# SSD steps hung beside the products of U, and y_a, s_out and w_o as a dense stage of their own

## The chip, the cores and the metric

The kernel runs on one core of one Trainium2 chip. The metric is the device time of one execution in microseconds. Before the change three runs took 2009.54, 2010.28 and 2015.11 us, a median of 2010.28 us.

TensorE is called PE below, VectorE DVE, ScalarE ACT and GpSimd POOL. SP is the engine whose queue issues all DMAs of this kernel, one after the other, in program order.

## The reference

One layer of a hybrid decoder block on 1024 tokens with 1024 channels, all in float32:

```python
u  = rmsnorm(h)
gate_a, gate_s, b_a, c_a, v_a, z, xbc, dt_raw = split(u @ w_in)
y_a = (b_a * causal_dwconv(c_a * v_a, conv_a_w)) @ w_a_out
xbc = silu(causal_dwconv(xbc, ssd_conv_w) + ssd_conv_b)
xs, bs, cs = split(xbc)
y   = ssd_chunked_scan(xs, dt, a, bs, cs) + d_skip * xs
y_s = group_rmsnorm(y * silu(z), ssd_norm_w) @ w_s_out
h   = h + (sigmoid(gate_a) * y_a + sigmoid(gate_s) * y_s) @ w_o
v   = rmsnorm(h)
h1, h3 = split(v @ w_up)
h   = h + (silu(causal_dwconv(h1) + b) * h3) @ w_down
out = rmsnorm(h)
```

The scan works in chunks of 128 tokens: within a chunk it multiplies the products of b and c by a lower triangular decay matrix exp(a_cum[l] - a_cum[s]) for each head; between chunks it carries a state of 64 x 128 per head. There are 32 heads of 64 channels in 4 groups, so 8 heads share a group's b and c. The group norm divides by the root mean square over the 512 channels of a group.

## The kernel before

**Products.** Each large product is made of float32 values that are split in a high part and a rest (`split` L136, `wsplit` L141: ACT casts the high part, POOL or DVE subtracts it for the low part). `product` (L240) accumulates hi x hi, hi x lo and lo x hi in one PSUM bank: twelve matmuls of 128x512. `Pair` (L252) multiplies two 128-column blocks of a weight with the operand U (later V) by a seven-product scheme: b11, b21, t1, t2, t3, t4, b22, so a pair is 84 matmuls. Raw weights come through four buffers (`load` L146, tag raw); split weights through 14 buffers of the tag w and four of wx.

**PSUM.** Eight banks: four have the name "mm" (`mm_tile`), four "sd" (`sd_tile`). Of a pair's products t1, t4 and b22 use sd, and so does every small product of the scan. A bank is free again when DVE or ACT has read it. The additions of a pair into its two results (L274 to L304) are on DVE.

**Order.** A tile scheduler takes program order as priority and places instructions on each engine's queue; an engine then executes its queue in order.

**Stages.** The row norms of x and the filling of U come first (`u_norm`, `fill_first`). Then come the pairs of U: xbc with its four-tap convolution on DVE (L508) and z, both stored to DRAM (`ssd_in`); then `ca_pairs` and the gates. Between those, `m_preps` calls `m_prep` 32 times, once for each group and chunk: it loads b and c (bc), forms their product pb (L585, in an sd bank), masks it on DVE (L587), forms the decays on ACT (Relu with a bias for each of 8 heads L591, Exp L592), multiplies both on DVE (L593) and stores the 128x1024 matrix to DRAM (md).

Then `steps` and `fill` weave 32 calls of `ssd_chunk`, each a generator of four pieces, with y_a and s_out. A chunk loads x, b, c, z (in) and the decay matrix (m), transposes x and b on PE (px L658, pb L660), scales them (xd L662 on DVE, xe L669 on ACT), and multiplies: pd = m x xd (L686), po = state x c (L696), pst = b x xe (L705). DVE and POOL sum y (L700 to L702) and the new state (L710, L714), DVE multiplies by z (L717), ACT squares (L718), and a product with a matrix of ones sums the squares (pn L723). Then a square root (L725), a reciprocal (L726), four scalings (L729) and the split into yh and yl follow, which s_out reads. `s_out` adds each group's product to sacc on DVE (L783).

`merge` joins both branches by the gates, `out_proj` (L853) multiplies by w_o and adds into h (L879). `v_norm` stores h to DRAM (hd), norms it, and `fill_first` and `fill_second` transpose it into V (pt_v, L176). The FFN's pairs then run; beside the first eleven, `w_sums` forms sums of w_down (tiles wd, L932) and stores them (td).

## Time and profile before

| | before |
|---|---|
| median of three runs | 2010.28 us |
| profiled execution | 2007.71 us |
| its span | 2006.0 us |
| mean granted TensorE clock | 0.986 of full |
| PE busy | 1923.7 us, 96% |
| DVE busy | 1395.0 us, 70% |
| POOL busy | 1215.7 us, 61% |
| ACT busy | 880.7 us, 44% |
| DMA | 346.84 MB, mean 173 GB/s |

The profiled execution lasts 1.71 us longer than its span, which runs from the first to the last instruction. Busy times are sums of an engine's instructions; a busy PE need not be at its peak, since matmuls overlap and their ends are modelled. A view by stretches shows for a piece of the span how long each engine was busy and with how many instructions. A row of waits names the engine that idled, the tile and line that it was about to work on, and the instruction that it waited for. Most tables and rows are quoted where the prediction uses them.

### The profile page before, as it was taken

What the parts mean: (1) busy time and instruction counts of PE and PEld (TensorE: products, weight loads), DVE (VectorE), ACT (ScalarE), POOL (GpSimd) and SP (SyncE); (2) the same over time, 40 slices, a digit from 0 to 9 for tenths busy, and PEclk for the clock granted to TensorE, in tenths of its full rate; (3) what the DMA queues carried; (4) which work ended last, traced back from release to release, by engine and by line L of the source; (5) the groups of instructions that cost most, each with busy time, mean ns of one, the idle gap of its engine ahead of it and who ended that gap; (6) DMA issues with size and microseconds to landing.
All of it is one profiled execution on the core that took longest, in us unless ns stands there. A gap on an engine that the chain in (4) does not pass through costs nothing. (4 is left out here: it accounts for less than half of the span.)

```text
span 2006.0 us, 26149 instructions
## 1 busy us (share of the span) xinstructions
PE 1923.7 (96%) x8978; PEld 1574.4 (78%) x8978; DVE 1395.0 (70%) x1732; ACT 880.7 (44%) x1676; POOL 1215.7 (61%) x895
## 2 busy tenths in 40 slices
...
GB/s 142 79 152 103 131 97 124 103 107 119 188 209 204 229 187 183 227 219 204 209 184 169 190 146 194 234 142 164 195 245 208 113 163 148 149 242 276 215 181 145
DMA packets 203573, 346.84 MB, mean 173 GB/s; under 512 B 14896, under 2 KB 111664, under 8 KB 203440
## 3 DMA queue, kind: packets, MB, share of 16 engines
...
## 5 line engine op out<-in xcount | busy, mean ns | idle before, releaser
L674 POOL TENSOR_TENSOR xs<-in,dsk 128x512 f32<-128x512 f32 x32 | 34.9, 1091 | 177.9 <-DMA in<-ssd_in 117.3
L508 DVE SCALAR_TENSOR_TENSOR cv<-xbc,scw,cv 128x1024 f32<-128x1024 f32 x72 | 109.8, 1551 | 15.8 <-ACT cv L504 15.8
L591 ACT ACTIVATE mp<-mp,tk 128x128 f32<-128x128 f32 x256 | 78.5, 389 | 93.4 <-DMA mp<-acd 79.5
L508 DVE SCALAR_TENSOR_TENSOR fcv<-fci,fcw,fcv 128x1024 f32<-128x1024 f32 x44 | 74.5, 1693 | 23.8 <-ACT fcv L504 23.6
L669 ACT ACTIVATE xe<-px,tk 128x64 f32<-128x64 f32 x256 | 56.1, 331 | 57.4 <-DVE xd L662 57.4
L246 PE MATMUL so<-yh,h_ws 128*128 128x512 f32 x256 | 77.0, 413 | 0.0
L246 PE MATMUL so<-yh,l_ws 128*128 128x512 f32 x256 | 73.2, 402 | 0.0
L246 PE MATMUL so<-yl,h_ws 128*128 128x512 f32 x256 | 73.2, 401 | 0.0
L593 DVE TENSOR_TENSOR mp<-mp,bc 128x1024 f32<-128x1024 f32 x32 | 51.8, 1620 | 27.7 <-ACT mp L592 27.6
L139 POOL TENSOR_TENSOR l_wo<-raw_wo,h_wo 128x512 fp32r<-128x512 f32 x24 | 37.4, 1566 | 39.0 <-PE so L246 25.5
L702 POOL TENSOR_TENSOR eb<-eb,xs 128x512 f32<-128x512 f32 x28 | 38.3, 1369 | 34.8 <-DVE eb L700 24.4
L246 PEld LDWEIGHTS so<-yl,h_ws 128*128 128x128 f32 x256 | 47.7, 188 | 12.6 <-issue 3.3
L246 PEld LDWEIGHTS so<-yh,l_ws 128*128 128x128 f32 x256 | 47.4, 188 | 11.9 <-issue 2.6
L246 PEld LDWEIGHTS so<-yh,h_ws 128*128 128x128 f32 x256 | 46.7, 188 | 12.6 <-issue 4.6
L718 ACT ACTIVATE xs<-eb 128x512 f32<-128x512 f32 x32 | 20.4, 639 | 74.3 <-DVE eb L717 74.3
L874 PE MATMUL wo<-h_wo,mh 128*128 128x512 f32 x128 | 50.3, 395 | 2.1 <-DVE sacc L783 0.8
L876 PE MATMUL wo<-h_wo,ml 128*128 128x512 f32 x128 | 50.1, 396 | 0.0
L875 PE MATMUL wo<-l_wo,mh 128*128 128x512 f32 x128 | 50.0, 392 | 0.0
L282 POOL TENSOR_TENSOR t1up<-raw_2up,raw_1up 128x512 f32<-128x512 f32 x22 | 36.7, 1666 | 17.3 <-DMA raw_2up<-in_w_up 10.9
L138 ACT CAST h_t4up<-t2up 128x512 fp32r<-128x512 f32 x22 | 13.7, 621 | 73.2 <-POOL t2up L300 46.6
L729 DVE SCALAR_TENSOR_TENSOR eb<-eb,wns,yr 128x128 f32<-128x128 f32 x128 | 44.8, 411 | 0.3
L981 ACT ACTIVATE fcv<-fcv 128x1024 f32<-128x1024 f32 x22 | 23.4, 1062 | 49.3 <-DVE fcv L508 49.3
...
## 6 DMA issues: line engine op xcount, KB each, us to landing
...
mp<-acd SPq DMA_DIRECT2D x32, 512.0 KB, 4.8
md<-mp SPq DMA_DIRECT2D x32, 512.0 KB, 3.0
m<-md SPq DMA_DIRECT2D x32, 512.0 KB, 5.0
ssd_in<-cv SPq DMA_DIRECT2D x24, 512.0 KB, 4.4
raw_wo<-in_w_o SPq DMA_DIRECT2D x24, 512.0 KB, 4.4
raw_1up<-in_w_up SPq DMA_DIRECT2D x22, 512.0 KB, 3.9
raw_2up<-in_w_up SPq DMA_DIRECT2D x22, 512.0 KB, 3.4
```

The lines of the kernel that those rows point to most:

```text
L139: (eng or pool).tensor_tensor(lo, v, f32(hi), op=ALU.subtract)
L246: pe.matmul(ps, wt[:, k, :], ct[:, k, :], start=(start and n == 0), stop=(stop and n == 11),)
L282: pool.tensor_tensor(self.t1, self.r2[:, :HALF], b11, op=ALU.subtract)
L508: dve.scalar_tensor_tensor(cv, ci[:, j : j + SEQ], w[:, j : j + 1], cv, op0=ALU.mult, op1=ALU.add)
L591: act.activation(m[:, h, :], m[:, h, :], AF.Relu, bias=a)
L593: dve.tensor_tensor(m, m, cb.unsqueeze(1).to_broadcast([P, HG, P]), op=ALU.mult)
L669: act.activation(xe[:, hc], px[:, hc], AF.Copy, scale=tk[:, 2, cc, q, g * HG + h : g * HG + h + 1],)
L702: pool.tensor_tensor(y, y, xs, op=ALU.add)
L729: dve.scalar_tensor_tensor(o, o, wns[:, 4 * g + j : 4 * g + j + 1], r, op0=ALU.mult, op1=ALU.mult)
L874: pe.matmul(pss[t], mh, wh, start=k == 0, stop=False)
L875: pe.matmul(pss[t], mh, wl, start=False, stop=False)
L876: pe.matmul(pss[t], ml, wh, start=False, stop=k == NK - 1)
```

## The change

**Steps beside the pairs.** `tick()` counts the products of pairs; `ssd_chunk` is cut into five pieces (loads, decay, transposes, the products, the norm's sum), and each piece of step s hangs at the product 11 + 6 s - 8, - 6, - 4, 0 or + 3, counted from the ninth pair. 29 of the pairs (BESIDE) run so, eight (BEFORE) ahead of them. **Decays in place.** The decay matrix is formed in a step, in the tile that the step reads; `m_prep` and md go. pc is the product of b and c that was pb in `m_prep`. **Rows in DRAM.** y goes to DRAM (yd) before the norm, and the norm's factor, one number a token and group, to rd. `y_half` loads both and scales while it fills s_out's operand. **Dense stage.** y_a, s_out and w_o run for each half of the tokens; s_out sums the four groups in one PSUM bank, and w_a_out and w_s_out (in another layout) are loaded once for each half. **w_sums** no longer lies in the FFN; in program order it stands beside s_out(0) and y_a(1). v takes a raw buffer, and the tag w has 11 buffers.

```diff
-NRAW, NW, NWX, NBIG, NB4, NC2, NT2, NROW = 4, 14, 4, 14, 3, 6, 3, 6
+NRAW, NW, NWX, NBIG, NB4, NC2, NT2, NROW = 4, 11, 4, 14, 3, 6, 3, 6
...
-XBC = (16, 18, 20, 22, 0, 2, 4, 6, 8, 10, 12, 14)
-Z_AFTER = (16, 18, 22, 0, 4, 6, 10, 12)
-PREP_CV, PREP_G = 3, 2
-YA = (0, 1, 2, 3, 4, 6, 8, 9)
-SLAG, LAST = 10, 31
+BEFORE = (
+    ("xb", 16), ("z", 0), ("xb", 18), ("z", 2), ("xb", 20), ("xb", 22), ("xb", 0), ("xb", 2),
+)
+BESIDE = (
+    ("xb", 4), ("z", 4), ("xb", 6), ("z", 6), ("ca", 0), ("ca", 1), ("ba", 0),
+    ("xb", 8), ("z", 8), ("xb", 10), ("z", 10), ("ca", 2), ("ca", 3), ("ba", 2),
+    ("xb", 12), ("z", 12), ("xb", 14), ("z", 14), ("ca", 4), ("ca", 5), ("ba", 4),
+    ("ca", 6), ("ca", 7), ("ba", 6), ("gs", 0), ("gs", 2), ("gs", 4), ("gs", 6), ("ga", 6),
+)
+D0, DSTEP = 11, 6
+LOADS, DECAY, TRANS, NORM = -8, -6, -4, 3
...
             product(ps, self.A[c], wsplit(v, f"{nm}{name}", eng, tag))
+            tick()
             return ps
...
+    slots, clock = {}, [None]
+    def tick():
+        if clock[0] is not None:
+            clock[0] += 1
+            for f in slots.pop(clock[0], ()):
+                f()
...
-    md = dram.tile([NG * NCH, P, SEQ], F32, name="md")
+    yd = [dram.tile([P, 4, SEQ], F32, name=f"yd{g}") for g in range(NG)]
+    rd = dram.tile([NG, NCH, P], F32, name="rd")
...
-            m_preps(PREP_CV)
...
-    def ssd_chunk(g, c, yh, yl):
+    states, stats = {}, {}
+    def ssd_chunk(s):
...
-        m = s4(f"m{nm}")[:, :SEQ]
-        sp.dma_start(m, md[g * NCH + c])
...
+        inp = ssp.tile([P, 6, P], F32, tag="in", name=f"in{nm}", bufs=2)
+        sp.dma_start(inp, xd_[g][:, 0:6, ts])
+        xt, bt, ct = inp[:, 0:4, :], inp[:, 4, :], inp[:, 5, :]
+        yield
+        m = ssp.tile([P, HG, P], F32, tag="m", name=f"m{nm}", bufs=1)
+        sp.dma_start(m, acd[hq, lq].unsqueeze(0).to_broadcast([P, HG, P]))
+        eb = c2(f"eb{nm}")
...
+        zt = ssp.tile([P, 4, P], F32, tag="z", name=f"zt{nm}", bufs=1)
+        sp.dma_start(zt, xd_[g][:, 6:10, ts])
+        for h in range(HG):
+            a = tk[:, 0, cc, q, g * HG + h : g * HG + h + 1]
+            act.activation(m[:, h, :], m[:, h, :], AF.Relu, bias=a)
+        act.activation(m, m, AF.Exp, scale=-1.0)
+        yield
 
...
+        pc = sd_tile(f"pc{nm}")[:, :P]
+        pe.matmul(pc, bt, ct, start=True, stop=True)
...
-        bk = row(f"bk{nm}", P)
+        bk = ssp.tile([P, P], F32, tag="bk", name=f"bk{nm}", bufs=1)
         act.copy(bk, pb)
+        cb = ssp.tile([P, P], F32, tag="cb", name=f"cb{nm}", bufs=1)
+        dve.tensor_tensor(cb, pc, tri, op=ALU.mult)
+        dve.tensor_tensor(m, m, cb.unsqueeze(1).to_broadcast([P, HG, P]), op=ALU.mult)
         yield
...
+        dve.tensor_tensor(xt, xt, tiles(pd), op=ALU.add)
+        if st is not None:
+            dve.tensor_tensor(eb, po, eb, op=ALU.mult)
+            pool.tensor_tensor(xt, xt, tiles(eb), op=ALU.add)
...
+        dve.tensor_tensor(xt, xt, zt, op=ALU.mult)
+        sp.dma_start(yd[g][:, :, ts], xt)
+        sq = eb
+        act.activation(sq, xt.rearrange("p j l -> p (j l)"), AF.Square)
+        dve.tensor_tensor(sq[:, : 2 * P], sq[:, : 2 * P], sq[:, 2 * P :], op=ALU.add)
+        dve.tensor_tensor(sq[:, :P], sq[:, :P], sq[:, P : 2 * P], op=ALU.add)
         yield
-        pn = sd_tile(f"pn{nm}")[:, :P]
-        pe.matmul(pn, ones, xs[:, :P], start=True, stop=True)
-        r = row(f"yr{nm}", P)
-        act.activation(r, pn, AF.Sqrt, scale=1.0 / HALF, bias=epsc)
-        dve.reciprocal(r, r)
-        for j in range(4):
-            o = tiles(y)[:, j, :]
-            dve.scalar_tensor_tensor(
-                o, o, wns[:, 4 * g + j : 4 * g + j + 1], r, op0=ALU.mult, op1=ALU.mult
-            )
-        split(tiles(y), yh[:, :, cs], yl[:, :, cs], dve)
+        pn = sd_tile(f"pn{nm}")[:, :1]
+        pe.matmul(pn, sq[:, :P], ones[:, :1], start=True, stop=True)
+        rs = tiny(f"yss{nm}")
+        dve.tensor_scalar(rs, pn, 1.0 / HALF, EPS, op0=ALU.mult, op1=ALU.add)
+        r = tiny(f"yr{nm}")
+        pool.tensor_tensor(r, rs, nhalf, op=ALU.pow)
+        sp.dma_start(rd[g, c].unsqueeze(1), r)
         yield
...
+    def at(n, f):
+        slots.setdefault(n, []).append(f)
+    NS = NG * NCH
+    for s in range(NS):
+        d = D0 + DSTEP * s
+        ch = ssd_chunk(s)
+        for o in (LOADS, DECAY, TRANS, 0, NORM):
+            at(d + o, lambda ch=ch: next(ch))
...
+    for item in BEFORE:
+        run(*item)
+    clock[0] = 0
+    for item in BESIDE:
+        run(*item)
+    while slots:
+        tick()
+    clock[0] = None
+    mixer.close()
...
+    def w_sums(k):
+        r, r2 = (s4(f"wd{f}{k}")[:, :SEQ] for f in range(2))
+        for f, t in enumerate((r, r2)):
+            sp.dma_start(t, w_down[f * KF + k])
+        b11, b12 = (r[:, h] for h in halves)
+        b21, b22 = (r2[:, h] for h in halves)
+        sub(b11, b12, b11)
...
+    def y_a(hf, ta, beside):
+        sl = halves[hf]
+        for j in range(NK):
+            raw = load(w_a_out[j], f"wa{hf}{j}")
+            ps = mm_tile(f"ya{hf}{j}")
             for q in range(2):
-                product(ps, ta[hf, q], ws[q], start=q == 0, stop=q == 1)
-            gh = t2(f"ga{j}{hf}")
+                w = wsplit(raw[:, halves[q]], f"wa{hf}{j}{q}", pool if q else dve)
+                product(ps, ta[q], w, start=q == 0, stop=q == 1)
...
+            beside(j)
+    def y_half(hf, res):
+        for g in range(NG):
+            rb = c2(f"rb{hf}{g}")
+            sp.dma_start(
+                rb,
+                rd[g].rearrange("c p -> (c p)")[halves[hf]].unsqueeze(0).to_broadcast([P, HALF]),
+            )
+            hi, lo = big_tile(f"yh{hf}{g}", F32R), big_tile(f"yl{hf}{g}", F32R)
+            res.append((hi, lo))
+            for j in range(0, 4, 2):
+                raw = load(yd[g][:, j : j + 2, halves[hf]], f"y{hf}{g}{j}").rearrange(
+                    "p (k t) -> p k t", k=2
+                )
+                for i in range(2):
+                    w = wns[:, 4 * g + j + i : 4 * g + j + i + 1]
+                    dve.scalar_tensor_tensor(
+                        raw[:, i, :], raw[:, i, :], w, rb, op0=ALU.mult, op1=ALU.mult
+                    )
+                split(raw, hi[:, j : j + 2, :], lo[:, j : j + 2, :], dve)
+                yield
+    def s_out(hf, ys, beside):
...
+            ps = mm_tile(f"so{hf}{j}")
+            for kk in range(2):
+                raw = load(w_s_out[kk * NK + j], f"ws{hf}{j}{kk}")
+                for i in range(2):
+                    g = 2 * kk + i
+                    w = wsplit(raw[:, halves[i]], f"ws{hf}{j}{g}", pool if i else dve)
+                    product(ps, ys[g], w, start=g == 0, stop=g == NG - 1)
+            gs, ma = c2(f"gs{hf}{j}"), c2(f"ma{hf}{j}")
+            sp.dma_start(gs, gsd[:, j, sl])
+            sp.dma_start(ma, mad[:, j, sl])
+            dve.scalar_tensor_tensor(gs, gs, 1.0, ps, op0=ALU.add, op1=ALU.mult)
+            dve.tensor_tensor(gs, gs, ma, op=ALU.add)
+            hi, lo = mg[j // 4]
+            split(gs, hi[:, j % 4, :], lo[:, j % 4, :])
+            beside(j)
+        return mg
...
     def v_norm(t):
         sp.dma_start(hd[t], hs[t])
-        v = b4(f"v{t}")
+        v = wp.tile([P, DM], F32, tag="raw", name=f"v{t}", bufs=NRAW)
...
+    def all_sums():
+        for k in range(KF):
+            w_sums(k)
+            yield
+    def beside(*gens):
+        return lambda j: [next(g, None) for g in gens]
+    sums = all_sums()
+    ta0, ta1, ys0, ys1 = [], [], [], []
+    for _ in ta_half(0, ta0):
+        pass
+    y_a(0, ta0, beside(y_half(0, ys0)))
+    mg0 = s_out(0, ys0, beside(ta_half(1, ta1), sums))
+    y_a(1, ta1, beside(y_half(1, ys1), sums))
     load_x(0)
-    out_proj(mg, 0, 4)
-    for n in range(LAST + 4, LAST + 8):
-        steps(n)
-        fill(n)
-    mg = merge(1)
+    out_proj(mg0, 0, 4)
+    def fill_beside(j):
+        if j % 2 == 0:
+            fill_first(V, v_norm(j // 2), j // 2, f"v{j // 2}")
+    V = operand("v")
+    mg = s_out(1, ys1, fill_beside)
...
-            w_sums(i)
```

Three places show how the rows moved on the engines. The first is PE around one SSD step. Before, in the scan of group 2, where so is a product of s_out:

```order
L246 MATMUL so100_9228<-yl10_8117,h_ws100_9224 128x512 x4
L705 MATMUL pst2_1_9202<-xe2_1_9082,bk2_1_9093 128x512
L246 MATMUL so100_9228<-yh10_8116,l_ws100_9225 128x512 x4
L246 MATMUL so101_9242<-yh14_8571,h_ws100_9224 128x512 x4
L246 MATMUL so101_9242<-yl14_8572,h_ws100_9224 128x512
L723 MATMUL pn2_0_9211<-xs2_0_8996,ones_662 128x128
L246 MATMUL so101_9242<-yl14_8572,h_ws100_9224 128x512 x3
```

After, group 0's second step among the products of an xbc pair of U:

```order
L256 MATMUL pt1xb6_2755<-us1h_301,l_t1xb6_2757 128x512 x4
L682 MATMUL pd0_1_2772<-m0_1_2589,xd0_1_2657 64x128 x8
L689 MATMUL po0_1_2781<-in0_1_2527,st0_2582 128x128 x4
L695 MATMUL pst0_1_2786<-xe0_1_2659,bk0_1_2669 128x512
L256 MATMUL pt2xb6_2814<-us2h_303,h_t2xb6_2815 128x512 x4
L256 MATMUL pt2xb6_2814<-us2l_304,h_t2xb6_2815 128x512 x4
L256 MATMUL pt2xb6_2814<-us2h_303,l_t2xb6_2816 128x512 x4
L256 MATMUL pt3xb6_2835<-us3h_305,h_t3xb6_2836 128x512 x4
L256 MATMUL pt3xb6_2835<-us3l_306,h_t3xb6_2836 128x512 x4
L256 MATMUL pt3xb6_2835<-us3h_305,l_t3xb6_2837 128x512 x4
L651 MATMUL px0_2_2852<-ident_75,in0_2_2727 128x128 x4
L653 MATMUL pb0_2_2857<-ident_75,in0_2_2727 128x128
```

The step's products pd, po and pst now stand in one piece between two products of a pair, and the next step's transposes follow two products later.

The second place is SP's queue where the last rows of h are stored (hd from h4 and h6) and weights of w_o (raw_wo) and of the FFN (raw_1up, raw_2up) are loaded. Before:

```order
L148 DMA raw_wo161_11834<-in_w_o 128x1024
L889 DMA hd_96<-h4_11348 128x1024
L148 DMA raw_wo162_11856<-in_w_o 128x1024
L889 DMA hd_96<-h4_11348 128x1024
L148 DMA raw_wo163_11878<-in_w_o 128x1024
L148 DMA raw_1up0_11922<-in_w_up 128x1024
L148 DMA raw_2up0_11961<-in_w_up 128x1024
L148 DMA raw_1up1_12031<-in_w_up 128x1024
L148 DMA raw_2up1_12070<-in_w_up 128x1024
L889 DMA hd_96<-h6_11350 128x1024 x2
```

After:

```order
L158 DMA raw_wo143_11774<-in_w_o 128x1024
L898 DMA hd_100<-h4_11600 128x1024 x2
L158 DMA raw_wo060_11818<-in_w_o 128x1024
L158 DMA raw_wo061_11840<-in_w_o 128x1024
L158 DMA raw_wo062_11862<-in_w_o 128x1024
L158 DMA raw_wo063_11884<-in_w_o 128x1024
L158 DMA raw_wo160_11972<-in_w_o 128x1024
L158 DMA raw_wo161_11994<-in_w_o 128x1024
L158 DMA raw_wo162_12016<-in_w_o 128x1024
L158 DMA raw_wo163_12038<-in_w_o 128x1024
L898 DMA hd_100<-h6_11602 128x1024 x2
L158 DMA raw_1up0_12082<-in_w_up 128x1024
```

Both stores of h4 now stand ahead of the weights wo06 and wo16, and both stores of h6 ahead of the FFN's first weight.

The third place is POOL in the last gate pairs (names with g) after the change:

```order
L149 TENSOR_TENSOR l_t2g10_8261<-t2g10_8239,h_t2g10_8260 128x512
L763 TENSOR_TENSOR wd00_9531<-wd10_9532,wd00_9531 128x512
L311 TENSOR_TENSOR t2g10_8239<-t2g10_8239,raw_1g10_8188 128x512
L724 TENSOR_TENSOR yr3_2_8006<-yss3_2_8004,nhalf_80 128x1
L763 TENSOR_TENSOR wd10_9532<-wd10_9532 128x512
L149 TENSOR_TENSOR l_t3g10_8324<-t3g10_8320,h_t3g10_8323 128x512
```

The sums of w_down (wd, L763) stand there among the splits of a gate pair and the scan's rows; before, all of them stood beside the FFN.

More of the change, by code (lines that the diff above doesn't have):

```diff
@@ L349, in tile_block @@
         fill_first(U, xs[t], t, f"u{t}")
+    rows_ = ExitStack()
+    tk = scm.tile([P, 3, 2, 4, NH], F32, name="tk")
+    cdb = scm.tile([P, 4, NH, 2], F32, name="cdb")
+    tri = scm.tile([P, P], F32, name="tri")
+    pool.memset(tri, 1.0)
+    pool.affine_select(
+        out=tri, in_=tri, compare_op=ALU.is_ge, fill=0.0, base=0,
+        pattern=[[1, P]], channel_multiplier=-1,
+    )
+    cur["row"] = rows_.enter_context(tc.tile_pool(name="rowp", bufs=1))
     dt_ps = sd_tile("ps_dt")[:, :QT]
@@ new lines, in run @@
+    def run(kind, i):
+        if kind == "xb":
+            xbc_pair(i)
+        elif kind == "z":
+            z_pair(i)
+        elif kind == "ca":
+            ca_pair(i)
+        elif kind == "ba":
+            ba_pair(i)
+        else:
+            gate_pair(*((GA, gad) if kind == "ga" else (GS, gsd)), i)
+    for item in BEFORE:
[7 more added lines that the diff above has]
+    mixer.close()
+    late = ExitStack()
@@ new lines, in tile_block, with sub, add @@
+    cur["x"] = late.enter_context(tc.tile_pool(name="scx", bufs=1))
+    def sub(o, p, q, eng=dve):
+        eng.tensor_tensor(o, p, q, op=ALU.subtract)
+    def add(o, p, q, eng=dve):
+        eng.tensor_tensor(o, p, q, op=ALU.add)
+    def w_sums(k):
[5 more added lines that the diff above has]
+        sub(b11, b12, b11)
+        sub(b12, b22, b12, pool)
+        sub(b22, b22, b11)
+        sub(b21, b22, b21, pool)
+        for i, t in enumerate((b11, b22, b12, b21)):
+            sp.dma_start(td[k, i], t)
@@ L739, in ta_half @@
+    def ta_half(hf, res):
         for q in range(2):
-            hi = big_tile(f"tah{hf}{q}", F32R)
-            lo = big_tile(f"tal{hf}{q}", F32R)
+            new = extra_tile if hf and q else big_tile
+            hi, lo = new(f"tah{hf}{q}", F32R), new(f"tal{hf}{q}", F32R)
+            res.append((hi, lo))
             for k in range(0, 4, 2):
@@ L747, in ta_half @@
                 split(raw, hi[:, k : k + 2, :], lo[:, k : k + 2, :], dve)
-            ta[hf, q] = (hi, lo)
-    def y_a(j):
-        raw = load(w_a_out[j], f"wa{j}")
-        ws = [
-            wsplit(raw[:, q * HALF : (q + 1) * HALF], f"wa{j}{q}")
-            for q in range(2)
-        ]
-        for hf in range(2):
-            sl = slice(hf * HALF, (hf + 1) * HALF)
-            ps = mm_tile(f"ya{j}{hf}")
+                yield
[4 more added lines that the diff above has]
+            ps = mm_tile(f"ya{hf}{j}")
             for q in range(2):
-                product(ps, ta[hf, q], ws[q], start=q == 0, stop=q == 1)
-            gh = t2(f"ga{j}{hf}")
+                w = wsplit(raw[:, halves[q]], f"wa{hf}{j}{q}", pool if q else dve)
+                product(ps, ta[q], w, start=q == 0, stop=q == 1)
+            gh = t2(f"ga{hf}{j}")
             sp.dma_start(gh, gad[:, j, sl])
@@ L765, in y_a @@
             sp.dma_start(mad[:, j, sl], gh)
-    sacc, sraw = {}, {}
-    def s_out(g, j, hfs):
-        if j % 2 == 0:
-            sraw[hfs] = load(w_s_out[4 * g + j // 2], f"ws{g}{j}{hfs[0]}")
-        jj = j % 2
-        w = wsplit(sraw[hfs][:, jj * HALF : (jj + 1) * HALF], f"ws{g}{j}{hfs[0]}", dve)
-        for hf in hfs:
-            ps = mm_tile(f"so{g}{j}{hf}")
-            product(ps, ys[g, hf], w)
-            if g == 0 and j % 4 == 0:
-                sacc[hf, j // 4] = big_tile(f"sacc{hf}{j // 4}")
-            acc = sacc[hf, j // 4][:, j % 4, :]
-            if g == 0:
-                act.copy(acc, ps)
-            else:
-                dve.tensor_tensor(acc, acc, ps, op=ALU.add)
```

216 lines of the change are left out of this document (45 added, 171 removed).

## The prediction

> **What bounds the kernel now.** I read the stretches table first, because the matrix products dominate and a stage without losses shows their price. Its columns are the stretch in us, its length, then for each engine the busy time with the number of instructions, the granted TensorE clock, the DMA share and GB/s.
>
> ```profile
> 100.00:500.00 400.00, 400.00 (x1769) 331.33 (x1768) 236.50 (x261) 175.60 (x245) 280.70 (x216) 1.00 0.35 117
> 500.00:775.00 275.00, 259.12 (x1138) 212.31 (x1137) 189.54 (x220) 165.48 (x390) 183.07 (x122) 0.98 0.65 210
> 775.00:850.00 75.00, 75.00 (x335) 62.14 (x334) 31.88 (x42) 33.05 (x47) 35.80 (x29) 1.00 0.54 176
> 850.00:1210.00 360.00, 349.53 (x2035) 277.15 (x2034) 273.86 (x498) 146.33 (x452) 119.83 (x103) 1.00 0.61 189
> 1210.00:1275.00 65.00, 64.07 (x282) 52.38 (x281) 39.48 (x49) 19.15 (x32) 22.95 (x15) 1.00 0.62 213
> 1275.00:1400.00 125.00, 107.90 (x469) 87.80 (x468) 111.33 (x115) 60.85 (x106) 101.12 (x71) 0.92 0.50 170
> 1400.00:1550.00 150.00, 140.31 (x599) 112.49 (x599) 110.67 (x111) 48.33 (x75) 130.06 (x92) 0.99 0.65 219
> 1550.00:1950.00 400.00, 400.00 (x1767) 331.20 (x1766) 281.34 (x271) 158.12 (x197) 254.86 (x178) 1.00 0.55 186
> ```
>
> In 100 to 500 and in 1550 to 1950 PE never idles: 400 / 1767 = 0.2264 us per 128x512 matmul, twelve of them a product. So PE bounds the kernel, and a stage can only gain what it spends beyond its matmuls at that price. To count the matmuls I took the same table for the product line L246 alone, then one undisturbed SSD step (all PE, then L246 alone).
>
> ```profile
> 500.00:775.00 275.00, 257.21 (x1074) 203.21 (x1073) 0.98 0.65 210
> 850.00:1210.00 360.00, 263.51 (x1024) 188.23 (x1023) 1.00 0.61 189
> 1275.00:1400.00 125.00, 53.17 (x213) 42.32 (x212) 0.92 0.50 170
> ```
>
> ```profile
> 1140.90:1148.96 8.06, 8.06 (x54) 1.00 0.62 161
> 1140.90:1148.96 8.06, 5.13 (x19) 3.58 (x19) 1.00 0.62 161
> ```
>
> The step took 8.06 us with 19 product matmuls, so its 35 small ones cost 8.06 - 19 x 0.2264 = 3.76 us, 0.107 each. With this the losses are:
> - 500 to 775: 275 - 1074 x 0.2264 - 64 x 0.107 = 25.0 us.
> - 850 to 1210: 360 - 1024 x 0.2264 - 1011 x 0.107 = 20.0 us.
> - 1210 to 1275: 65 - 282 x 0.2264 = 1.2 us.
> - 1275 to 1400: 64 of the 469 are transposes, so 125 - 405 x 0.2264 - 64 x 0.107 = 26.5 us.
> - 1400 to 1550: 150 - 599 x 0.2264 = 14.4 us.
>
> Then the table of waits (total us, how often, the longest) says what PE waited for there.
>
> ```profile
> PE pb L585 <- DVE ba L299: 8.1, 3, 3.4
> PE pt_v L176 <- DVE rs_v L165: 7.9, 2, 5.7
> PE pb L585 <- DVE cc L302: 7.7, 3, 3.3
> PE po L696 <- ACT yr L725: 6.8, 7, 1.5
> PE pt4up L246 <- POOL fci L915: 4.5, 1, 4.5
> PE pt_v L176 <- DVE v L168: 4.4, 2, 2.5
> PE pb21up L246 <- DVE fci L274: 2.8, 3, 1.3
> PE pt1up L246 <- ACT vs1h L138: 2.3, 1, 2.3
> ```
>
> The two pb rows are the decay matrices' small product, which waits for a PSUM bank of the group "sd" that DVE still has to read: six waits, 15.8 us. The rest of that stage's 25.0 is the clock at 0.98 and smaller gaps. The po row, 6.8 us, is the same kind of wait in the SSD, for the bank that the norm's square root (L725) still reads.
>
> **The change part by part.** *The separate stages go.* The SSD no longer runs among y_a and s_out, and no decay matrix is made between pairs, so the losses of 500 to 775, 850 to 1210 and 1210 to 1275 go: **-46.2 us**. The small matmuls stay: 32 steps of 3.76 us, and pc, which was pb in the old preparation, moves with them.
>
> *What takes their place* is one stage of 29 pairs (29 x 7 x 12 = 2436 product matmuls, 551.5 us) and some 32 x 3.4 = 108 us of small ones, 660 us, and the question is what it loses. DVE and POOL must carry the steps' work beside the pairs':
>
> ```profile
> L662 DVE TENSOR_TENSOR xd<-px,tk 128x512 f32<-128x512 f32 x32 | 21.2, 663 | 8.3 <-PE px L658 8.3
> L700 DVE TENSOR_TENSOR eb<-po,eb 128x512 f32<-128x512 f32 x28 | 19.1, 682 | 5.5 <-DMA eb<-ead 5.5
> L701 DVE TENSOR_TENSOR xs<-xs,pd 128x512 f32<-128x512 f32 x28 | 18.9, 674 | 0.0
> L714 DVE TENSOR_TENSOR st<-st,pst 128x512 f32<-128x512 f32 x24 | 16.3, 681 | 9.4 <-POOL st L710 9.1 <-PE pst L705 0.2
> L717 DVE TENSOR_TENSOR eb<-eb,in 128x512 f32<-128x512 f32 x32 | 23.7, 739 | 11.7 <-POOL eb L702 11.6
> L719 DVE TENSOR_TENSOR xs<-xs 128x256 f32<-128x256 f32 x32 | 14.5, 453 | 11.1 <-ACT xs L718 10.7
> L720 DVE TENSOR_TENSOR xs<-xs 128x128 f32<-128x128 f32 x32 | 10.5, 330 | 0.7
> L674 POOL TENSOR_TENSOR xs<-in,dsk 128x512 f32<-128x512 f32 x32 | 34.9, 1091 | 177.9 <-DMA in<-ssd_in 117.3
> L702 POOL TENSOR_TENSOR eb<-eb,xs 128x512 f32<-128x512 f32 x28 | 38.3, 1369 | 34.8 <-DVE eb L700 24.4
> L710 POOL TENSOR_TENSOR st<-st,cdb 128x512 f32<-128x512 f32 x24 | 26.3, 1096 | 0.0
> L669 ACT ACTIVATE xe<-px,tk 128x64 f32<-128x64 f32 x256 | 56.1, 331 | 57.4 <-DVE xd L662 57.4
> L593 DVE TENSOR_TENSOR mp<-mp,bc x32: 1207/1574/2306, 512.9 to 760.3; 128x1024 f32<-128x1024 f32 x32
> L508 DVE SCALAR_TENSOR_TENSOR cv<-xbc,scw,cv 128x1024 f32<-128x1024 f32 x72 | 109.8, 1551 | 15.8 <-ACT cv L504 15.8
> L592 ACT ACT_TABLE_LOAD  x1: 1283/1283/1283, 501.9 to 501.9; - x1
> ```
>
> DVE's first seven rows add up to 124.2 us, POOL's to 99.5. All U pairs with the old preparation lie between 100 and 850: DVE 236.5 + 189.5 + 31.9 = 457.9, POOL 499.6, ACT 374.1 us. The order shows seven of the eleven w_down sums in the last gate pairs, some 24 us of POOL. The new stretch is about 750 - 25 + 108 = 833 us, so DVE stands at (457.9 + 124.2) / 833 = 70%, POOL at (499.6 + 99.5 + 24) / 833 = 75%. ACT with xe, some 30 us of squares and copies, and 17 more table loads of 1.28 us is at 58%. The rows above have both outcomes at such shares: DVE 70% and POOL 64% without a loss in 1550 to 1950; DVE 69% and POOL 67% with 9% lost in 500 to 775; DVE 74% and POOL 87% with 10% lost in 1400 to 1550. So the share alone doesn't decide; how long a bank waits for DVE does. Six waits of 2.6 us came with 32 preparations of two DVE instructions, in bursts of two or three. Now 32 steps come singly, one every six products, but each holds five more banks. I take twice the waits and twice the loss beside them that does not show as a wait: **+30 us**. The bounds are 0 (100 to 500 and 1550 to 1950) and 9% of the stage, 660 x 0.0909 / 0.9091 = 66 us (as in 500 to 775). The square root's wait, the reciprocal, the 128x128 scalings and the yl split leave the step, so nothing there is as late as L725 was; next in line are xs+pd, po x eb and st+pst, which hold pd, po and pst for 2.0 us of DVE together.
>
> *The memory trips.* 32 stores and 32 loads of decay matrices go; 32 stores of y and of its row factors, 24 loads of them, and w_a_out and w_s_out read a second time come. The DMA share is 0.65 at most in any stretch, and y is read by its first user tens of us after its store, since y_a(0) or s_out(0) lies between. I cost these at nothing. If loads came late, the raw buffers would hold the dense stage, which is the next term.
>
> *The dense stage.* A y_a block is 24 matmuls, 5.43 us. In that time DVE has a lo subtraction, a gate product, two scalings by the rows and a 128x1024 lo subtraction. By the 0.68 us of rows like L701 (a 1024-wide one counted twice) that is 4.1 us, and with each an extra half for meeting POOL 6.1. So 16 blocks lose between 0 and 16 x 0.7 = 11; waiting for raw buffers could add half as much, 17. I take **+5 us**, nearer the free end, because s_out with its 10.9 us blocks has slack to catch up. The 48 sums into sacc go from DVE, which wasn't waited for there: nothing.
>
> *FFN.* The sums of w_down leave the first eleven pairs.
>
> ```profile
> L932 DVE TENSOR_TENSOR wd<-wd,wd x11: 679/1765/1798, 1369.5 to 1532.2; 128x512 f32<-128x512 f32 x11
> L932 POOL TENSOR_TENSOR wd<-wd x11: 1283/1740/2273, 1371.3 to 1535.1; 128x512 f32<-128x512 f32 x11
> ```
>
> Each pair loses two POOL instructions of about 1.5 us and two of DVE; in 1400 to 1550, with some nine pairs, POOL falls from 130 to about 103 us, 69%, near the 64% of the stretch behind it, which loses nothing. Of its 14.4 us loss I take **-11**, with bounds 0 and -14.4, because the 4.5 us wait for fci may partly stay.
>
> *The tail, 1275 to 1400.* Direct waits are 7.9 + 4.4 + 2.3 = 14.6 of its 26.5 us. The first four V fills now lie beside s_out(1), which hides the 4.4. But in SP's queue the stores of h4 and h6 now stand ahead of the next weights, so those loads start only behind the last h sum:
>
> ```profile
> raw_wo<-in_w_o SPq DMA_DIRECT2D x24, 512.0 KB, 4.4
> raw_1up<-in_w_up SPq DMA_DIRECT2D x22, 512.0 KB, 3.9
> ```
>
> With a cast and a lo subtraction that is about 6 us, twice, against 5.7 at most for the one such gap now, during which transposes run. 14.6 becomes about 12: **-2 us**, with bounds -11 (the loads are early after all) and +8 (both gaps come on top, with the lower clock of 0.92 behind them).
>
> *The norm's sum, pn,* is one column wide instead of 128: of 64 x 0.107 = 6.8 us I take **-2**, with bounds 0 (the weight load stays and may set the pace) and -6.8. The Trainium skill, "TensorE: Matmul & The Clock Gate", section "Back-to-back issue gap", gives about 25 ns for 1 to 64 columns; by it the term would be -5 and the forecast 3 us lower. No one-column matmul is in this trace.
>
> **Sum:** -46.2 + 30 + 5 - 11 - 2 - 2 = -26 us on a span of 2006.0: 1980. The profiled execution took 2007.71 us, 1.7 more than its span, so 1982; it is 2.6 us under the median of 2010.28, inside the three runs' spread of 5.6.
>
> **The rivals.**
> - *Nothing is lost beside the pairs* (0 instead of 30): **1952**. For it: 800 us of this trace run at 100% with DVE at 59 to 70%. Against it: where something extra hung between pairs, 9% was lost.
> - *The new stage goes as 500 to 775 did*, over all its length, because DVE and POOL together are as full (66 instead of 30): **2018**. For it: shares of 70 and 75% against 69 and 67%. Against it: that stage's losses were mostly six waits. The Trainium skill, "SBUF — State Buffer", section "SBUF: two separate sides", has a mechanism: a DVE instruction with two SBUF inputs and a POOL instruction exclude each other at one port pair for their whole length. An estimate by that rule: nine POOL instructions of 1.28 and two of DVE at 0.68 per pair are 374 us, the steps' about 180, taps, gates and sums about 115, so some 670 us against PE's 660, and the loss would be at least 10. The spread of the wd rows, 679 to 1798 ns, is what it would look like.
> - *Slower: every step waits for its bank.* Place: the first of px, pd, po or pst finds all four "sd" banks waiting for DVE behind a 1.55 us tap or the 1.2 to 2.3 us decay product in DVE's queue. Price: a wait of 15.8 / 6 = 2.6 us in each of 32 steps, 84 us, with 2% more for the clock, 97: **2049**. It decides from 30 + 26 = 56 us of loss, 1.75 us a step. For it: the two longest waits were 3.3 and 3.4. Against: a wait in six of 32, when two or three preparations came at once.
> - *The dense stage waits* for raw buffers or DVE at the upper bound (17 instead of 5): **1994**.
>
> **How the numbers follow.** Forecast 0.55 (own range 1960 to 2004), nothing lost 0.11, dense stage 0.07, as 500 to 775 0.16, a wait in every step 0.11. A measurement of this kernel can tell 0.3%, 6 us around 2010, from no change. Faster: nearly all of the first three, 0.72; same: most of the fourth, 0.12; slower: the last and a part of the fourth, 0.16. The range runs from 1948 to 2020: below it lie only added lower bounds, above it the waits in every step and a piece of the fourth.
>
> **What would show it.** Right: between the eighth U pair and the first y_a block PE busy is 95% or more, its waits at px, pd, po and pst sum to 10 to 30 us, no stretch of FFN pairs loses more than 3%, and two gaps of about 6 us lie at pt_v of tokens 4 and 6. Wrong: waits of 2 us in most steps, POOL at 90% beside the pairs, a granted clock under 0.97 there, or y_a blocks spaced over 6 us.

## The result, and the profile after

The changed kernel took 2118.23 us, the median of four runs (2114.95 to 2121.95), against 2012.69 us of four runs of the kernel before. The ratio is 1.0523, 95% interval 1.0494 to 1.0553: slower by 5.2%, where 1982 us had been forecast. The span of the profiled execution is 2116.3 us, 110.3 us more than before.

The same table of stretches, after. The pairs with the SSD steps beside them end at 1076, y_a and s_out for the first half and y_a for the second at 1265, s_out for the second half with parts of w_o at 1400, the tail before the FFN at 1500.

```profile
275.00:1076.00 801.00, 700.73 (x3406) 554.54 (x3406) 505.87 (x646) 375.78 (x888) 504.23 (x389) 0.93 0.66 150
1076.00:1265.00 189.00, 185.00 (x796) 151.06 (x797) 118.41 (x134) 65.75 (x100) 79.85 (x54) 0.98 0.84 290
1265.00:1400.00 135.00, 135.00 (x613) 112.08 (x612) 46.08 (x65) 42.65 (x72) 49.15 (x38) 1.00 0.48 160
1400.00:1500.00 100.00, 80.64 (x310) 62.08 (x309) 62.44 (x69) 40.57 (x72) 56.73 (x42) 0.86 0.30 101
1500.00:2060.00 560.00, 560.00 (x2472) 463.70 (x2471) 368.71 (x379) 217.81 (x284) 361.51 (x265) 1.00 0.48 163
```

The products (L256) alone:

```profile
275.00:1076.00 801.00, 609.43 (x2328) 456.36 (x2328) 0.93 0.66 150
1076.00:1265.00 189.00, 184.88 (x792) 150.29 (x792) 0.98 0.84 290
```

By the prices of the prediction (0.2264 us a large matmul, 0.107 a small one):
- 275 to 1076 loses 801 - 2328 x 0.2264 - 1078 x 0.107 = **158.6 us**, where 30 had been forecast. PE idles 100.3 us of it (801 - 700.7); the other 58 are busy time above these prices, at a granted clock of 0.93. The other engines are not full there: DVE 63%, POOL 63%, ACT 47%.
- 1076 to 1265 loses 189 - 792 x 0.2264 = 9.7 us, where 5 had been forecast.
- 1400 to 1500 holds 32 transposes and 278 large matmuls and loses 33.6 us, against 26.5 for the tail before.
- 1500 to 2060 loses nothing (560 / 2472 = 0.2265). The FFN's 14.4 us are gone.

Together -46.2 + 158.6 + 9.7 + 7.1 - 14.4 = +115 us, against the 110 of the spans. So all of the loss is in the stage where the steps hang beside the pairs. PE's longest waits say little of it, only that banks and casts come late from ACT:

```profile
PE pn L720 <- ACT bk L672: 19.5, 5, 6.3
PE pn L720 <- issue: 15.1, 5, 6.8
PE pn L720 <- ACT m L646: 8.1, 1, 8.1
```

The waits of all engines (total us, times, longest) say more. ACT's Relu on the decay tile waits for that tile's load in every one of the 32 steps, and DVE then waits for ACT's square, which stands behind the Relu on ACT's queue:

```profile
ACT m L645 <- DMA m<-acd: 278.9, 32, 14.5
DVE eb L716 <- ACT eb L715: 124.2, 24, 10.7
```

No other load holds an engine for nearly as long: the next row of this kind is 30.0 us, for w_down (wd). Before, the same Relu had waited 79.5 us (the last number of the row, behind what it waited for):

```profile
L591 ACT ACTIVATE mp<-mp,tk 128x128 f32<-128x128 f32 x256 | 78.5, 389 | 93.4 <-DMA mp<-acd 79.5
```

In the list of DMAs (KB each, median us from issue to landing) this load takes nearly twice the 4.8 us of the same load before (mp from acd, the first row), and a store of half a kilobyte, the row factors, takes as long:

```profile
mp<-acd SPq DMA_DIRECT2D x32, 512.0 KB, 4.8
m<-acd SPq DMA_DIRECT2D x32, 512.0 KB, 9.0
rd<-yr SPq DMA_DIRECT2D x32, 0.5 KB, 8.8
```

Two steps side by side on SP's queue and on ACT (start, duration, instruction):

```profile
610.77 0.33 SPq L725 DMA_DIRECT2D rd<-yr  x1
611.19 1.25 SPq L636 DMA_DIRECT2D eb<-ead  x2
615.61 0.38 SPq L631 DMA_DIRECT2D m<-acd  x1
```

```profile
624.27 1.87 ACT L645 ACTIVATE m<-m,tk 128x128 f32<-128x128 f32 x6 [9.07 <-DMA m<-acd]
```

```profile
638.34 0.37 SPq L631 DMA_DIRECT2D m<-acd  x1
643.48 0.34 SPq L725 DMA_DIRECT2D rd<-yr  x1
```

In the first step m's load was issued 4.8 us behind a store to rd, and Relu could start 8.7 us after it, with ACT idle for 9.07. That store landed after 7.7 us, at 618.5; from 612 to 618 the DMA engines moved 10 GB/s, though two loads of eb and later m were under way, and from 620 to 626, behind the landing, 271. In the second step the store came behind the load; the load landed in 3.8 us, the least of all 32. By the starts in the trace a store stood less than 9 us ahead of m's load in 28 of the 32 steps; those loads took a median of 9.7 us, the other four 4.9.

### The profile page after: what moved, and what is told of

Its sections match the earlier page's. It is cut to its first block, busy times and chain, and to the rows that moved or that the text cites. A ratio compares the mean times of both kernels' runs of the same rounds, so it can differ in the third digit from the quotient of the medians.

```text
span 2116.3 us, 26130 instructions
## 1 busy us (share of the span) xinstructions
PE 1965.7 (93%) x8978; PEld 1596.9 (75%) x8978; DVE 1341.5 (63%) x1580; ACT 896.8 (42%) x1669; POOL 1263.9 (60%) x959
## 3 DMA queue, kind: packets, MB, share of 16 engines
q1 hardware_dynamic: 216176, 336.80, 54.9%
## 4 chain that ended last, share of the span: by engine, by line
PE 69%; DMA 15%; DVE 6%; ACT 5%; issue 2%; POOL 2%; SPq 1%; POOLq 0%; ACTq 0%; DVEq 0%
PE so L256 8%; DMA m<-acd 7%; PE d L1000 3%; PE d L1001 3%; PE d L1002 3%; PE ya L256 3%; DMA td<-wd 3%; PE pt2up L256 3%; PE pt4up L256 3%; PE pb22up L256 3%; PE pt3up L256 3%; PE pb11up L256 3%; PE pb21up L256 3%; PE pt1up L256 3%; ACT m L645 2%
## 5 line engine op out<-in xcount | busy, mean ns | idle before, releaser
L645 ACT ACTIVATE m<-m,tk 128x128 f32<-128x128 f32 x256 | 78.5, 389 | 278.9 <-DMA m<-acd 278.9
L716 DVE TENSOR_TENSOR eb<-eb 128x256 f32<-128x256 f32 x32 | 21.4, 670 | 124.3 <-ACT eb L715 124.2
L149 POOL TENSOR_TENSOR l_ws<-raw_ws,h_ws 128x512 fp32r<-128x512 f32 x32 | 47.2, 1483 | 61.4 <-PE so L256 26.6
L148 ACT CAST h_ws<-raw_ws 128x512 fp32r<-128x512 f32 x64 | 38.3, 620 | 77.2 <-PE so L256 53.2
L256 PE MATMUL so<-yh,h_ws 128*128 128x512 f32 x256 | 69.0, 391 | 0.0
L256 PE MATMUL so<-yh,l_ws 128*128 128x512 f32 x256 | 68.6, 390 | 0.3 <-DVE l_ws L149 0.3
L256 PE MATMUL so<-yl,h_ws 128*128 128x512 f32 x256 | 68.5, 389 | 0.0
L675 DVE TENSOR_TENSOR m<-m,cb 128x1024 f32<-128x1024 f32 x32 | 55.8, 1745 | 10.4 <-ACT m L646 9.7
L149 POOL TENSOR_TENSOR l_wa<-raw_wa,h_wa 128x512 fp32r<-128x512 f32 x16 | 26.2, 1638 | 60.3 <-ACT h_wa L148 44.7
L149 DVE TENSOR_TENSOR l_ws<-raw_ws,h_ws 128x512 fp32r<-128x512 f32 x32 | 28.5, 895 | 50.1 <-PE so L256 27.5
L256 PEld LDWEIGHTS so<-yh,l_ws 128*128 128x128 f32 x256 | 48.0, 188 | 10.7 <-DVE l_ws L149 0.7
L256 PEld LDWEIGHTS so<-yl,h_ws 128*128 128x128 f32 x256 | 48.0, 188 | 10.1
L256 PEld LDWEIGHTS so<-yh,h_ws 128*128 128x128 f32 x256 | 47.8, 188 | 9.7
L720 PE MATMUL pn<-ones,eb 128*128 128x1 f32 x64 | 11.8, 253 | 46.4 <-ACT bk L672 19.5
L720 PEld LDWEIGHTS pn<-ones,eb 128*128 128x128 f32 x64 | 13.3, 229 | 53.9 <-ACT bk L672 21.6
L712 DVE TENSOR_TENSOR in<-in,zt 128x512 f32<-128x512 f32 x32 | 40.7, 1273 | 17.2 <-POOL in L699 17.1
```

Of the source, the lines that this page charges most:

```text
L148: act.copy(hi, v)
L149: (eng or pool).tensor_tensor(lo, v, f32(hi), op=ALU.subtract)
L256: pe.matmul(ps, wt[:, k, :], ct[:, k, :], start=(start and n == 0), stop=(stop and n == 11),)
L645: act.activation(m[:, h, :], m[:, h, :], AF.Relu, bias=a)
L675: dve.tensor_tensor(m, m, cb.unsqueeze(1).to_broadcast([P, HG, P]), op=ALU.mult)
L712: dve.tensor_tensor(xt, xt, zt, op=ALU.mult)
```

## The experiments

Four theories were held, one after the other. A: m has one buffer, so its load waits for the step before, and ACT, which works in order, stands at Relu with all casts behind it. B: DVE and POOL are too full, or exclude each other. C: eleven buffers for split weights are too few. D: the store of the row factors, 128 pieces of 4 bytes, holds up what is issued behind it. Medians are given with the ratio to the kernel before on the same chip and its 95% interval. m's landing is the median of the list of DMAs, ACT's wait the row for m.

### A second buffer for m, and its control

```diff
-NRAW, NW, NWX, NBIG, NB4, NC2, NT2, NROW = 4, 11, 4, 14, 3, 6, 3, 6
+NRAW, NW, NWX, NBIG, NB4, NC2, NT2, NROW = 4, 9, 4, 14, 3, 6, 3, 6
...
-        m = ssp.tile([P, HG, P], F32, tag="m", name=f"m{nm}", bufs=1)
+        m = ssp.tile([P, HG, P], F32, tag="m", name=f"m{nm}", bufs=2)
```

> Edit: the decay tile m gets a second buffer; to make room the split weights' tag w gets 9 buffers instead of 11. Theory A (the load of m can start only when the step before has read m, and ACT then idles 8.7 us a step with all casts behind it): ACT's wait for m<-acd falls from 279 us to under 60, the stage beside the pairs loses 45 to 75 us instead of 159, time 2005 to 2040. Theory B (DVE and POOL together are too full, or exclude each other): the wait moves but the loss stays, time above 2085. Theory C (too few buffers for split weights): slower than the changed kernel.

Measured: 2186.85 us, 1.0881 (1.0862 to 1.0900). The control has the first of the two lines alone:

> Control for e1: only the tag w with 9 buffers instead of 11, m with one buffer. Theories A and B: within 6 us of the changed kernel, 2112 to 2124. Theory C: slower by 15 us or more.

Measured: 2136.76 us, 1.0640 (1.0613 to 1.0667).

```profile
ACT m L645 <- DMA m<-acd: 282.6, 27, 19.0
```

That is the first of the two runs. The load could now be issued one step earlier, but the scheduler put Relu earlier too (a median of 41 us ahead of the step's first pd instead of 13.5, by the starts in the traces), m's landing rose to 11.0 us, and ACT waited as long as with one buffer. Against the control the second buffer costs 50 us; so one buffer is not what makes the kernel slow. Two split buffers fewer cost 18.5 us: theory C has a price, but whether 14 would give back as much wasn't tried.

### Relu later, and m's neighbours away

The first edit moves Relu and Exp two products later, the second moves the loads of eb and zt there instead.

```diff
         sp.dma_start(m, acd[hq, lq].unsqueeze(0).to_broadcast([P, HG, P]))
...
-        for h in range(HG):
-            a = tk[:, 0, cc, q, g * HG + h : g * HG + h + 1]
-            act.activation(m[:, h, :], m[:, h, :], AF.Relu, bias=a)
-        act.activation(m, m, AF.Exp, scale=-1.0)
         yield
...
         pe.matmul(pc, bt, ct, start=True, stop=True)
+        for h in range(HG):
+            a = tk[:, 0, cc, q, g * HG + h : g * HG + h + 1]
+            act.activation(m[:, h, :], m[:, h, :], AF.Relu, bias=a)
+        act.activation(m, m, AF.Exp, scale=-1.0)
```

> Edit: m keeps one buffer and its load stays at its place, but ACT's Relu and Exp on it move two products (5.4 us) later, into the piece of the transposes. Theory A: each of ACT's waits shrinks by up to 5.4 us, from 279 to 110 to 160 us in sum; the decay product then comes later, so pd may wait; time 2040 to 2085. Theory B: no change, 2110 to 2125.

Measured: 2102.65 us, 1.0470 (1.0448 to 1.0492); ACT's wait 245 us, since the scheduler drew Relu forward again: it starts a median of 13.6 us ahead of pd, 13.5 without the edit.

> Edit: the loads of eb and zt, which follow m's load on the same queue, move two products later; m keeps one buffer. If m's 9.0 us from issue to landing come of these neighbours, it lands in 5 to 6 us as the old preparation's (4.8), ACT's wait falls by some 100 us and the time to 2050 to 2080. If they don't, m stays at 8 to 9 us and the time within 10 us of 2118.

Measured: 2124.54 us, 1.0579 (1.0558 to 1.0600); m lands in 9.0 us as before the edit. But the scheduler hardly moved the neighbours: a load of zt was issued while m's was under way in 20 steps without the edit and in 17 with it, one of eb in 4 and in 9. So the run doesn't rule them out; the run with eight stores below does, where the order behind m is much the same and m lands in 5.0 us. That leaves what stands ahead of m's load.

### Relu held back

```diff
+        with tc.issue_after(cast[0].ins):
+            for h in range(HG):
+                a = tk[:, 0, cc, q, g * HG + h : g * HG + h + 1]
+                act.activation(m[:, h, :], m[:, h, :], AF.Relu, bias=a)
+            act.activation(m, m, AF.Exp, scale=-1.0)
         dve.tensor_tensor(m, m, cb.unsqueeze(1).to_broadcast([P, HG, P]), op=ALU.mult)
```

Here cast[0] is ACT's last cast of a weight; the piece stands one product ahead of pd.

> Edit: Relu, Exp and the decay product of a step stand one product ahead of pd, and Relu is held behind the cast of that product on ACT, so the scheduler can't draw it forward as it did in e3. Stores and m as changed. Theory A (ACT stands at Relu with all its casts behind it while m is on its way): even with 9 us of landing the wait on m falls from 279 to under 140 us, time 2035 to 2085. Theory B (DVE and POOL): 2105 to 2130, whatever ACT's wait does.

Measured: 2101.10 us, 1.0460 (1.0431 to 1.0489); ACT's wait 229 us, m lands in 8.8. It is 17 us faster, but the hold didn't do what it was meant to: Relu still starts 13.9 us ahead of pd. So neither this run nor the one with Relu later tells what ACT's order is worth, and theory A stays open by them.

### The factors as one piece: a new cost in its place

```diff
-        pn = sd_tile(f"pn{nm}")[:, :1]
-        pe.matmul(pn, sq[:, :P], ones[:, :1], start=True, stop=True)
+        pn = sd_tile(f"pn{nm}")[:1, :P]
+        pe.matmul(pn, ones[:, :1], sq[:, :P], start=True, stop=True)
...
-        pool.tensor_tensor(r, rs, nhalf, op=ALU.pow)
-        sp.dma_start(rd[g, c].unsqueeze(1), r)
+        pool.tensor_tensor(r, r, nhalf[:1].to_broadcast([1, P]), op=ALU.pow)
+        sp.dma_start(rd[g, c].unsqueeze(0), r)
```

> Edit: the norm's sum is formed as a row of 128 on one partition (ones as the one stationary column), and the factors go to rd as one piece of 512 bytes instead of 128 pieces of 4. Everything else as changed. Theory D (the store of 4-byte pieces takes 8.8 us and holds up what is issued behind it, above all m's load): m lands in 4 to 5.5 us instead of 9.0, ACT's wait on it falls from 279 to 110 to 160 us, the time to 2010 to 2070. Theory A alone (one buffer for m and ACT's order, whatever the store): m stays near 9 us, time 2105 to 2125.

Measured: 2427.09 us, 1.2047 (1.2020 to 1.2074). The run with Relu two products later besides:

> Edit: e5 and e3 together: row store, and Relu and Exp two products later. Theory D: with m landing in 4 to 5.5 us the two products cover it, ACT's wait falls under 80 us, time 2000 to 2050, at least 10 us below e5. If the scheduler draws Relu forward again, as in e3, within 16 us of e5.

Measured: 2423.70 us, 1.2031 (1.1994 to 1.2069). Both forecasts of the time miss. The groups of the first show a new cost (times in ns: least, median, most):

```profile
L723 POOL TENSOR_TENSOR yr<-yr,nhalf x32: 20706/20717/21587, 309.4 to 1415.1; 1x128 f32<-1x128 f32 x32
```

POOL's power of 128 values in one partition takes 20.7 us, 32 of them 663 us. The changed kernel's, one value in each of 128 partitions, takes 0.55. That it makes up the 309 us above the changed kernel is likely, but not shown: no run takes this cost out alone.

Of the store the first run does tell something. Its landings aren't on record, but Relu can't start before m has landed, and it starts a median of 4.4 us after the issue of m's load, where the changed kernel's starts after 9.1. So 32 stores of one piece each leave m's load in time, as theory D has it, and ACT's wait on it falls to 173 us. The queue's packets bear it out (packets, MB, share of the time of 16 DMA engines), first in the changed kernel, then here, with 32 stores of one piece:

```profile
q1 hardware_dynamic: 216176, 336.80, 54.9%
q1 hardware_dynamic: 211632, 336.80, 41.8%
```

Of 2116.3 us the first share is 1162 us, of 2425.3 the second 1014, with the same bytes.

### The kernel before with the small store added

A store of 128 pieces of 4 bytes ahead of each decay matrix's load, which nothing reads. The first version left its place to the scheduler, the second holds it.

```diff
-        sp.dma_start(bc, xd_[g][:, 4:6, c * P : (c + 1) * P])
+        bl = sp.dma_start(bc, xd_[g][:, 4:6, c * P : (c + 1) * P])
...
-        sp.dma_start(m, acd[hq, lq].unsqueeze(0).to_broadcast([P, HG, P]))
+        with tc.issue_after(bl.ins):
+            sl = sp.dma_start(rd[i].unsqueeze(1), ones[:, :1])
+        with tc.issue_after(sl.ins):
+            sp.dma_start(m, acd[hq, lq].unsqueeze(0).to_broadcast([P, HG, P]))
```

> The kernel before, with one store of 128 pieces of 4 bytes to DRAM ahead of each decay matrix's load in its 32 preparations; nothing reads it. Theory D: mp<-acd goes from a median of 3.5 us to 8 or more, ACT's wait on it from 79 to 180 us or more, and the kernel gets 15 to 80 us slower (2025 to 2090). If such a store is harmless, mp stays under 5 us and the time within 6 us of 2010.

Measured for the first version: 2015.36 us, 1.0017 (1.0000 to 1.0033). All 32 stores were issued between 22.4 and 51.2 us, where no decay matrix is loaded: the order of SP's queue is the scheduler's, not the program's. So this run didn't test what it was made for. The second version:

> The kernel before, with a store of 128 pieces of 4 bytes in each of the 32 preparations, held between the load of b and c and the decay matrix's load on SP's queue; nothing reads it. Theory D: mp<-acd goes from a median of 3.5 us to 6 or more, ACT's wait on it from 71 to 79 us to over 120, time 2020 to 2080. If such a store is harmless in itself: mp under 5 us and 2005 to 2017 us.

Measured: 2110.08 us, 1.0500 (1.0480 to 1.0521), **101 us** slower, more than expected. The 3.5 us in both expectations is the median over loads of the tile and stores out of it together; the loads alone take the 4.8 us of the list, and 7.9 is to be compared with that.

```profile
mp<-acd SPq DMA_DIRECT2D x32, 512.0 KB, 7.9
rd<-ones SPq DMA_DIRECT2D x32, 0.5 KB, 9.5
```

```profile
ACT mp L595 <- DMA mp<-acd: 191.2, 24, 17.7
PE pb L589 <- DVE pr L299: 56.3, 7, 15.7
```

ACT's wait on the load rises from 79.5 to 191 us. 32 stores of 512 bytes make the kernel before nearly as slow as the changed one, without any other part of the change. The hold alone, without the store, has no run.

### Eight stores instead of 32, and the stores behind m

The factors stay in a column of rall; every fourth chunk four columns are turned into rows, and go out as four pieces of 512 bytes.

```diff
-        r = tiny(f"yr{nm}")
+        r = rall[:, s : s + 1]
         pool.tensor_tensor(r, rs, nhalf, op=ALU.pow)
-        sp.dma_start(rd[g, c].unsqueeze(1), r)
+        yield
+        if c % 4 == 3:
+            pr = sd_tile(f"pr{nm}")[:4, :P]
+            pe.transpose(pr, rall[:, s - 3 : s + 1], ident)
+            rt = ssp.tile([4, P], F32, tag="rt", name=f"rt{nm}", bufs=1)
+            dve.tensor_scalar(rt, pr, 1.0, None, op0=ALU.mult)
+            sp.dma_start(rd[g, c - 3 : c + 1], rt)
         yield
...
-        for o in (LOADS, DECAY, TRANS, 0, NORM):
+        for o in (LOADS, DECAY, TRANS, 0, NORM, 7):
```

> Edit: the norm's factors stay in SBUF; after every fourth chunk four columns are turned into rows on PE and go to rd as four pieces of 512 bytes, 8 stores in all instead of 32 with 128 pieces of 4 bytes. Theory D (those stores hold up m's load behind them): m lands in 4 to 5.5 us instead of 9.0, ACT's wait on it falls from 279 to 120 to 180 us, the time to 2020 to 2080. If the stores are harmless: m stays at 8 to 10 us, time 2105 to 2130.

Measured: **1999.00 us**, 0.9950 (0.9930 to 0.9970): 119 us below the changed kernel, and 0.5% faster than the one before.

```profile
ACT m L646 <- DMA m<-acd: 133.6, 29, 11.0
```

```profile
m<-acd SPq DMA_DIRECT2D x32, 512.0 KB, 5.0
```

```profile
275.00:970.00 695.00, 671.66 (x3442) 536.85 (x3442) 525.79 (x664) 379.97 (x891) 516.11 (x392) 0.99 0.56 177
275.00:970.00 695.00, 585.24 (x2355) 439.30 (x2355) 0.99 0.56 177
```

The stage is 106 us shorter. It loses 695 - 2355 x 0.2264 - 1087 x 0.107 = 45.5 us instead of 158.6, with DVE at 76% and POOL at 74%, more than in the slow kernel: they had been waiting, not full.

Part of this gain may not come from the landing. In the changed kernel SP's queue also stood still at the store itself until POOL had made the factors:

```profile
SPq L725 <- POOL yr L724: 72.8, 21, 8.2
```

What that wait costs isn't separated here. The stores added to the kernel before read a constant and wait for nothing on POOL, and they cost 101 us all the same.

The other way keeps all 32 stores and only holds each behind the next load of m (kept in mload):

```diff
+            with tc.issue_after(mload[s + 2].ins):
+                sp.dma_start(rd[g, c].unsqueeze(1), r)
```

> Edit: the 32 small stores stay, but each is issued right behind the next load of m instead of right ahead of it. Theory D: m lands in 4 to 5.5 us, ACT's wait falls by 80 us or more, the time to 2025 to 2090; what is issued behind the store now lands late instead (the raw weights). If the stores are harmless: 2105 to 2130.

Measured: 2056.65 us, 1.0239 (1.0176 to 1.0301), from two runs of 2046.89 and 2066.41. About half of the loss is gone. m lands in 5.5 us, and ACT's wait on it is 177 us. Other loads stay as late as in the changed kernel: zt takes 5.9 us (5.3 there, 3.4 with eight stores), a pair's second weight (raw_2cv) 7.3 (7.6 there, 3.8 with eight). So the stores had delayed more than m; how the other half divides among these loads and the rest of ACT's wait isn't separated.

### Both: eight stores and Relu held back

> Edit: e8 and e10 together. Theories A and D: m lands in 4 to 5.5 us and Relu comes some 4 us behind its issue, so ACT's wait on m falls under 60 us, the stage beside the pairs loses 30 to 70 us instead of 159, time 1990 to 2035. Theory B: still above 2085.

Measured: 1999.00 us, 0.9951 (0.9931 to 0.9970), the same as with eight stores alone. ACT's wait is 131 us, not under 60 as expected: the hold again hardly moved Relu (13.7 us ahead of pd, 13.3 without it). So the run doesn't tell what the rest of that wait costs.

### v out of the raw buffers

```diff
-        v = wp.tile([P, DM], F32, tag="raw", name=f"v{t}", bufs=NRAW)
+        v = s4(f"v{t}")[:, :DM]
```

> Edit: e8, and v lies in the buffers s4 instead of the raw weights' buffers, so that the last weights of w_o and the first of the FFN are issued ahead of the stores of h again. If v in raw buffers is what the tail pays for: the 100 us behind the first transposes of tokens 4 and 5 lose 12 to 25 us instead of 33, time 1983 to 1993. If the tail is the chain from h to V itself: 1995 to 2003.

Measured, on top of the eight stores: **1985.83 us**, 0.9878 (0.9864 to 0.9893), 13 us better, and the fastest of all. SP's waits in the 100 us of the tail, first with v in the raw buffers:

```profile
SPq L905 <- DVE h L895: 30.5, 3, 16.1
SPq L158 <- PE pt_v L186: 12.1, 3, 10.1
```

and with v elsewhere:

```profile
SPq L905 <- DVE h L895: 11.6, 4, 10.9
```

```profile
1285.00:1385.00 100.00, 80.79 (x325) 62.07 (x324) 64.20 (x70) 41.38 (x73) 59.56 (x43) 0.91 0.30 107
1285.00:1385.00 100.00, 87.70 (x373) 70.63 (x373) 76.19 (x81) 48.81 (x81) 78.59 (x57) 0.91 0.32 116
```

The first row is the run with eight stores, the second this one. Weights are no longer loaded into a buffer that v holds until its transposes (L186). On SP's queue two loads of w_o instead of eight now follow the stores of h4, and four weights of the FFN are loaded ahead of the stores of h6, where none was. With 32 transposes in each, the stretch loses 30.2 and 19.4 us.

## Why the prediction was wrong

- **The memory trips, costed at nothing: the step that failed.** The prediction counted bytes and the DMA share, and asked only whether y would be there in time for its reader. The stores of the row factors carry 16 KB in all, but each takes 8.8 us, and what is issued behind it comes late; in this order that is m's load, in 28 of 32 steps, and ACT stands at Relu until it lands. Eight stores instead of 32 take 119 us away, 32 such stores cost the kernel before 101: shown from both sides. That it is the pieces and not the number of stores shows in the run with 32 stores of one piece, where m is in time. The Trainium skill, "DMA: Bandwidth & Descriptors", section "Queues, rings and completion order", says that each DMA engine takes the descriptors of an issuing engine in the order of the ring; the 9.0 us of m behind the store, against 5.0 without and 5.5 ahead of it, agree. The section "Latency and other measured facts" of that page of the Trainium skill speaks of a fixed cost of about 2 us for a DMA. The 8.8 us of 512 bytes in 128 pieces are far above it, and the measurement decides.
- **The signs.** Of the prediction's own signs of being wrong, a granted clock under 0.97 beside the pairs came: 0.93. PE was busy 87% of the stage there, not 95%. Its waits at px, pd, po and pst add up to 6.8 us, less than the 10 to 30 forecast; it waited at pn instead, 46.4 us, which no sign named.
- **Lost beside the pairs, 30 us forecast.** Without the small stores 45.5: half as much again, inside the 0 to 66 that were given. The term looked only at DVE and POOL. ACT's row for the same load before, with 79.5 us of idle time, stood in the list of groups and wasn't weighed.
- **The rivals.** The slower one had PE wait for a bank in each step, 97 us, at DVE's queue. The direction was right and the size too small, 97 against 158.6; the place was ACT's queue, and the cause a load. That DVE and POOL are full is refuted as the cause of the slowdown by the run with eight stores, where both are busy for a larger share of the stage and the time falls. Whether they cause some of the 45.5 us left there wasn't tried.
- **The stages that go, -46.2 us,** and the SSD's small matmuls at 3.76 us a step: with them, the kernel with eight stores adds up: -46.2 + 45.5 + 8.2 for the dense stage + 3.8 for the tail - 14.4 = -3 us, against -6.5 between the spans.
- **The norm's sum, -2 us.** By the starts in the trace the two one-column matmuls of a step lie a median of 0.07 us apart and the next matmul 0.11 behind, 32 x 0.18 = 5.7 us instead of 6.8: about -1.
- **The dense stage, 5 us:** 9.7 measured, inside its bounds. **FFN, -11:** all 14.4 came.
- **The tail, -2 us, had the wrong sign:** +7, inside its bounds. The order of the stores of h was seen, but not why: v takes the raw buffers. Without that it loses 19.4 us in its 100, 14 less than in the changed kernel.
- With these two causes gone the kernel takes 1985.8 us, 4 from the forecast. That is partly luck: its stage beside the pairs still loses 695 - 2373 x 0.2264 - 1087 x 0.107 = 41.4 us instead of 30, and a better tail, the whole of the FFN's 14.4 and some 5 us that no term explains make up for it.

Not settled is why the pieces take so long, and whether their number, 128, or their size, 4 bytes, sets the 8.8 us.
